# One half chunk in twelve converted on GpSimd, beside the split of x, and expert 0 in another order: a layer with sixteen experts on one core

## The chip, the core and the metric

The kernel runs on one core of one Trainium2 chip. The metric is device time in microseconds (us) of one launch; the median of three runs counts. The profile names the engines PE (TensorE's matmuls), PEld (its weight loads), DVE (VectorE), ACT (ScalarE), POOL (GpSimd) and SP (SyncE, which here only issues DMAs).

## What is computed

One transformer layer over 1024 latent tokens of width 1024 (with 256 context tokens): a combined input projection, neighbourhood attention and a gated token MLP, an output projection, and then a mixture of 16 experts in which each token goes to 2. Only the expert part and the routing ahead of it are touched here:

```python
gate = (one_hot(g_idx) ... * within ...).reshape(-1, N_EXPERTS)    # two nonzeros per token
out = jnp.zeros_like(t)
for e in range(N_EXPERTS):                                          # 16
    hid = jax.nn.silu(t @ w1[e]) * (t @ w3[e])                      # 1024 -> 512
    out = out + gate[:, e:e + 1] * (hid @ w2[e])                    # 512 -> 1024
```

## The kernel before

**Split arithmetic.** Each float32 operand of a matmul is split into a high part (rounded by a copy to the matmul's format) and a low part (the rest, by a subtraction). `mm3` issues three matmuls for each product: high by high (L86), high of x by low of the weight (L87), low of x by high of the weight (L88). Splitting x means: transpose on PE into PSUM, `hi` on ACT, `lo` on DVE.

**Weights.** An expert's weights come in six chunks of 128x2048; chunk g = 6e + c. Chunks 0 and 1 hold w1 and w3 for the first half (f=0) of the hidden columns, 2 and 3 for the second (f=1), 4 and 5 hold w2. A chunk is loaded by SP's queue into one of seven raw slots (`raw`; the one that lies in an older tile shows as `acc`), and is then converted in two halves of 128x1024: `e_hi` makes `chi` on ACT (L941), `e_lo` makes `clo` by a subtraction of two SBUF tiles (L946) on DVE or on POOL. When a chunk's conversion is through, `e_load` puts the load of chunk g+7 into the slot. The six pairs `chi`/`clo` are used in turn, so chunk g+6 overwrites chunk g.

**One expert.** The first 128 tokens of an expert are its first tile. Its rows are gathered two experts ahead into `gf` by an indirect DMA on POOL's queue, and x is split (`x_split(0)`, tiles `yhi`, `ylo`) one expert ahead. Tokens beyond 128 make a second tile (`xhi`, `xlo`, `hB`); up to 64 of them are worked with both parts stacked in one operand (`half_...`, L1401 writes its low part). How many tokens an expert has is read at run time, and the second tile's work stands in branches. In order: `x_more(e,1)` splits the second tile; `h_mm(e,0,0)` is f=0 of the first tile (24 matmuls into PSUM tile `b`); the conversion of chunks 4 and 5; `more1(e)`, all the rest of the second tile; `h_mm(e,0,1)` is f=1, with a hook after its third step; `x_split(0)` for the next expert; `gather(e+2,0)`; `y_mm` multiplies by w2 (into `yb`), its first quarter, then `h_T(0,1)`, then the rest; `y_out` scales by the gate on DVE (L1387) and adds to the output by an indirect DMA. `h_T` transposes the hidden tile `hA` on PE (L1367), with `hhi` on ACT (L1369) and `hlo` on DVE (L1370).

**PSUM.** The transposes of `h_T(0,f)` and of both halves of `x_split(0)` share two PSUM buffers of the pool `pst4` in turn: h_T(0,0) takes the first, x's first half the second, x's second half the first again, h_T(0,1) the second again. So x's second half waits for `hlo` of h_T(0,0), and h_T(0,1) waits for `ylo` of x's first half.

**What sets the order.** From the last routing tile on, every engine runs its instructions in the order in which the code is written (`manual_schedule`). Ahead of that, in the output projection and routing (`o_post`, `route`, with chunks 0 and 1 converted among them), a list scheduler orders each engine, so that a moved instruction can move others. In routing a tile's norm goes DVE, POOL (a power, L83), DVE (`hf`, L1005; logits, L1066), then a chain of small DVE operations to `mb` (L1089), which PE needs for `pr` (L1092).

**Experts by size in this input.** Experts 1, 3 to 9 and 14 have one tile; 0, 2 and 12 a half second tile; 10, 11, 13 and 15 a full second tile (15 a half third one as well).

Of the kernel before, what the change touches and what calls it, by code (L numbers as in the profile page):

```python
# [15 lines left out]
AF = mybir.ActivationFunctionType  # L16
# [12 lines left out]
E = 16  # L29
# [10 lines left out]
def hybrid_layer_kernel(ctx, tc, a, out):  # L40
    nc = tc.nc
# [43 lines left out]
    def mm3(po, xh, xl, wh, wl, first, last):  # L85
        nc.tensor.matmul(po, xh, wh, start=first, stop=False)  # L86
        nc.tensor.matmul(po, xh, wl, start=False, stop=False)  # L87
        nc.tensor.matmul(po, xl, wh, start=False, stop=last)  # L88
# [806 lines left out]
    NS, NR = 6, 7  # L895
# [5 lines left out]
    raw = [rawp.tile([P, 2048], F32, name=f"raw{i}") for i in range(3)]  # L901

    def slot_of(g):
        return g if g < 3 else g - 3 if g < 5 else g - 2 if g < 9 else slot_of(g - NR)
    sl0 = ctx.enter_context(pool("sl0"))
    chi = [sl0.tile([P, 2048], F32R, name=f"chi{i}") for i in range(2)]
# [4 lines left out]
    def e_load(g, eng=nc.sync):  # L911
        if g >= CH:
            return
        if held:
            held.append(g)
            return
        w_chunk(*divmod(g, 6), raw[slot_of(g)], eng)
# [10 lines left out]
    def e_conv(g, i, eng=None):  # L928
        if g >= CH:
            return  # L930
        e_hi(g, i)
        if eng is None:
            eng = nc.gpsimd if g == 7 or i == 1 and (g == 6 or g >= 2 * 6 and g % 6 in (0, 5)) else nc.vector
        e_lo(g, i, eng)

    def e_hi(g, i):
        sl = slice(i * 1024, (i + 1) * 1024)
        if g == 7:
            nc.vector.tensor_copy(chi[g % NS][:, sl], raw[slot_of(g)][:, sl])
        else:  # L940
            nc.scalar.activation(chi[g % NS][:, sl], raw[slot_of(g)][:, sl], AF.Copy)  # L941

    def e_lo(g, i, eng):
        sl = slice(i * 1024, (i + 1) * 1024)
        r, hi, lo = raw[slot_of(g)], chi[g % NS], clo[g % NS]
        eng.tensor_tensor(lo[:, sl], r[:, sl], hi[:, sl].bitcast(F32), op=ALU.subtract)  # L946
        if i == 1:
            e_load(g + NR if g > 1 else g + 3)

    es_r = ExitStack()  # L950
# [320 lines left out]
    for q in range(2):  # L1271
        sl = slice(q * 4, q * 4 + 4)
# [34 lines left out]
    def wk(e, c, k):  # L1307
        g = 6 * e + c
        n = 512 if c < 4 else 1024
        return chi[g % NS][:, k * n:(k + 1) * n], clo[g % NS][:, k * n:(k + 1) * n]  # L1310
# [4 lines left out]
    def bank(j, first):  # L1315
        if j:
            return psy.tile([P, 512], F32, tag="y", name="yb")
        return first.tile([P, 512], F32, tag="b", name="b")

    def bank4(j):  # L1320
        return bank(j, pst).rearrange("p (a n) -> p a n", a=4)
# [10 lines left out]
    def gather(e, j, n=P):  # L1332
        xg = (sc_f, xgi, xg2)[min(j, 2)]
        nc.gpsimd.indirect_dma_start(out=xg[0:n, :], out_offset=None, in_=hfD[:, :],  # L1334
                                     in_offset=bass.IndirectOffsetOnAxis(ap=lt[0:n, e, j, 0:1], axis=0))
        return xg

    def x_split(j):
        xg = (sc_f, xgi, xg2)[min(j, 2)]
        hi, lo = (xTi, xT0)[min(j, 1)]  # L1340
        for q in range(2):
            tr = bank4(j)
            for i in range(4):
                k = q * 4 + i
                nc.tensor.transpose(tr[:, i, :], xg[:, k * P:(k + 1) * P], ident)
            sl = slice(q * 4, q * 4 + 4)
            nc.scalar.activation(hi[:, sl, :], tr, AF.Copy)
            nc.vector.tensor_tensor(lo[:, sl, :], tr, hi[:, sl, :].bitcast(F32), op=ALU.subtract)  # L1348

    def h_mm(e, j, f, hook=None):  # L1350
        hi, lo = (xTi, xT0)[min(j, 1)]
        po = bank(j, psh)
        for k in range(KD):
            wh, wl = wk(e, 2 * f + k // 4, k % 4)
            mm3(po, hi[:, k, :], lo[:, k, :], wh, wl, k == 0, k == KD - 1)
            if hook is not None and k == hook[0]:
                hook[1]()
        h = (hA, hB)[min(j, 1)]
        nc.scalar.activation(h, po[:, 0:256], AF.Silu)
        nc.vector.tensor_tensor(h, h, po[:, 256:512], op=ALU.mult)  # L1360

    def h_T(j, f):
        hi, lo = hTs[min(j, 1)]
        h = (hA, hB)[min(j, 1)]
        tr = bank4(j)
        for i in range(2):
            nc.tensor.transpose(tr[:, i, :], h[:, i * P:(i + 1) * P], ident)  # L1367
        sl = slice(f * 2, f * 2 + 2)
        nc.scalar.activation(hi[:, sl, :], tr[:, 0:2, :], AF.Copy)  # L1369
        nc.vector.tensor_tensor(lo[:, sl, :], tr[:, 0:2, :], hi[:, sl, :].bitcast(F32), op=ALU.subtract)  # L1370

    def y_mm(e, j, k0, k1):
        hi, lo = hTs[min(j, 1)]
        if k0 == 0:
            yss[j] = [bank(1, psy) for _ in range(2)]
        for k in range(k0, k1):
            wh, wl = wk(e, 4 + k // 2, k % 2)
            for i in range(2):
                sl = slice(i * 512, (i + 1) * 512)
                mm3(yss[j][i], hi[:, k, :], lo[:, k, :], wh[:, sl], wl[:, sl], k == 0, k == 3)  # L1380

    def y_out(e, j):
        y = yo[min(j, 1)]
        gate = lt[:, e, j, 1:2].bitcast(F32)
        for i in range(2):
            sl = slice(i * 512, (i + 1) * 512)
            nc.vector.scalar_tensor_tensor(y[:, sl], yss[j][i], gate, g_f[:, sl], op0=ALU.mult, op1=ALU.mult)  # L1387
        nc.gpsimd.indirect_dma_start(out=out[:, :], out_offset=bass.IndirectOffsetOnAxis(ap=lt[:, e, j, 0:1], axis=0),  # L1388
                                     in_=y, in_offset=None, compute_op=ALU.add)
# [22 lines left out]
    def half_h(e, j, f, hook=None):  # L1412
        po = bank(1, psy)
        for k in range(KD):
            wh, wl = wk(e, 2 * f + k // 4, k % 4)
            nc.tensor.matmul(po, xT0[0][:, k, :], wh, start=k == 0, stop=False)
            nc.tensor.matmul(po, xT0[0][:, k, :], wl, start=False, stop=k == KD - 1)
            if hook is not None and k == hook[0]:
                hook[1]()
        s = xg2[0:HP, f * 512:(f + 1) * 512]  # L1420
        half_sum(s, po)
        h = hB[0:HP, :]
        nc.scalar.activation(h, s[:, 0:256], AF.Silu)
        nc.vector.tensor_tensor(h, h, s[:, 256:512], op=ALU.mult)
# [29 lines left out]
    def conv2(g):  # L1454
        for i in range(2):
            e_conv(g, i)
# [3 lines left out]
    def count(e):  # L1460
        if e <= E:
            cr[e] = nc.values_load(cnt[0:1, e:e + 1], min_val=0, max_val=T)  # L1462

    def gather_more(e):
        if e < E:
            with tc.If(cr[e] > P):
                gather(e, 1)


    def second(e, j, one, other):  # L1470
        with tc.If(cr[e] > P * j + HP) as c:
            one()
        with c.Else():
            other()

    def x_more(e, j):
        second(e, j, lambda: x_split(j), lambda: half_x(j))

    def full(e, j):
        h_mm(e, j, 1, (2, lambda: h_T(j, 0)))  # L1480
        y_mm(e, j, 0, 1)
        h_T(j, 1)
        y_mm(e, j, 1, 4)
        y_out(e, j)

    def half(e, j):
        half_h(e, j, 1, (6, lambda: half_hT(0)))
        half_y(e, j, 0, 2)
        half_hT(1)
        half_y(e, j, 2, 4)  # L1490
        half_out(e, j)
# [54 lines left out]
    for e in range(E):  # L1546
        g0 = 6 * e
        count(e + 1)
        if e == 0:
            y_mm(0, 0, 0, 4)  # L1550
            y_out(0, 0)
            gather_more(1)
            with tc.If(cr[0] > P):
                second(0, 1, lambda: h_mm(0, 1, 0), lambda: half_h(0, 1, 0))
            conv2(6)
            conv2(7)
            with tc.If(cr[0] > P):
                second(0, 1, lambda: full(0, 1), lambda: half(0, 1))
            x_split(0)
            gather(2, 0)  # L1560
            conv2(8)
            conv2(9)
            continue
        with tc.If(cr[e] > P):
            x_more(e, 1)
        h_mm(e, 0, 0)
        gather_more(e + 1)
        conv2(g0 + 4)
        conv2(g0 + 5)
        more1(e)  # L1570

        def b_hook():
            h_T(0, 0)
            conv2(g0 + 6)
        h_mm(e, 0, 1, (2, b_hook))
        if e + 1 < E:
            x_split(0)
        if e + 2 < E:
            gather(e + 2, 0)
        y_mm(e, 0, 0, 1)  # L1580
        h_T(0, 1)
        conv2(g0 + 7)
        y_mm(e, 0, 1, 4)
        conv2(g0 + 8)
        y_out(e, 0)
        conv2(g0 + 9)
# [102 lines left out]
```

## Time and profile before

| what | value |
|---|---|
| median of three runs (lowest, highest) | 1068.91 us (1068.53, 1077.0) |
| the profiled execution's own time | 1073.15 us |
| its span (first to last instruction) | 1071.3 us |
| PE busy | 1004.6 us, 94% of the span |
| DVE, ACT, POOL busy | 735.4, 536.3, 381.6 us |
| low parts made on DVE and on POOL (L946) | 160 and 32 halves |
| read from and written to HBM | 210.45 and 43.29 MB |

The span leaves out 1.85 us around the first and last instruction, and the profiled execution took 4.24 us longer than the median. Terms worked out from the trace are differences; they are added to the profiled time and to the median alike.

### The profile page before, as it was taken

Reading aid. Unit: us, or ns where it says so; the run is one execution under the profiler, and the core shown is the slowest. Engines: PE = TensorE matmul, PEld = TensorE weight load, DVE = VectorE, ACT = ScalarE, POOL = GpSimd, SP = SyncE. Lnnn points to the kernel's source line nnn. Section 1 sums busy time; section 2 is a strip of 40 time slices with the busy share of each in tenths; the row PEclk is TensorE's granted clock in tenths of the full one; section 3 lists DMA queues with packets and bytes.
Section 4 is the critical chain, followed back from the end, with each engine's and each line's share of the span. In section 5 each row is a group of like instructions: output and inputs, shape, how many; then the busy total and the mean of one; then the engine's idle time right before and its main releaser. Section 6 shows DMA issues by size and latency. Waiting matters only on the chain. (4 is left out here: it accounts for less than half of the span.)

```text
span 1071.3 us, 15841 instructions
## 1 busy us (share of the span) xinstructions
PE 1004.6 (94%) x5161; PEld 816.6 (76%) x5161; DVE 735.4 (69%) x1478; ACT 536.3 (50%) x1024; POOL 381.6 (36%) x311
## 2 busy tenths in 40 slices
PE   9999899999999999999999888999998999999992
PEld 4688787876888989988888766777776888787771
DVE  2677658874627989967776858688888654765821
ACT  4643125243527989854322437476676543554611
POOL 1130321232302565641223554435645423243510
PEclk9999999999999999999999999999999999999997
DMA  9793605876757797959342698799999996886431
GB/s 325 271 316 134 200 1 177 287 237 243 252 210 263 253 352 265 322 182 324 122 149 80 202 299 287 247 332 353 346 360 353 343 294 201 292 257 194 131 60 16
DMA packets 138118, 255.26 MB, mean 238 GB/s; under 512 B 10310, under 2 KB 86726, under 8 KB 137994
## 3 DMA queue, kind: packets, MB, share of 16 engines
q1 hardware_dynamic: 122876, 201.57, 55.7%
q0 software_dynamic: 15120, 52.19, 16.1%
q8 instruction: 60, 0.98, 0.4%
q14 instruction: 62, 0.51, 0.2%
HBM read 210.45 MB, written 43.29 MB: 237 GB/s over the span
## 5 line engine op out<-in xcount | busy, mean ns | idle before, releaser
L946 DVE TENSOR_TENSOR clo<-raw,chi 128x1024 fp32r<-128x1024 f32 x140 | 174.2, 1291 | 18.8 <-ACT chi L941 17.7
L941 ACT ACTIVATE chi<-raw 128x1024 fp32r<-128x1024 f32 x166 | 162.6, 1049 | 1.5 <-DMA raw<-in_w 1.3
L86 PE MATMUL po<-whi,hhi 128*128 128x512 f32 x352 | 146.0, 415 | 0.0
L87 PE MATMUL po<-wlo,hhi 128*128 128x512 f32 x352 | 139.6, 397 | 0.0
L88 PE MATMUL po<-whi,hlo 128*128 128x512 f32 x352 | 139.3, 396 | 0.0
L1388 POOL DMA_INDIRECT out<-xb,lt x20 | 58.0, 2899 | 152.0 <-DVE xb L1387 152.0
L86 PE MATMUL b<-chi,yhi 128*128 128x512 f32 x256 | 104.7, 409 | 7.0 <-PEq L1528 4.1
L88 PE MATMUL b<-chi,ylo 128*128 128x512 f32 x256 | 101.7, 397 | 2.0 <-DVE ylo L1348 1.6
L87 PE MATMUL b<-clo,yhi 128*128 128x512 f32 x256 | 101.3, 396 | 0.0
L83 POOL TENSOR_TENSOR ss<-ss,nhalf 128x1 f32<-128x1 f32 (+1 forms) x36 | 46.0, 1276 | 144.2 <-DVE ss L82 144.0
L946 POOL TENSOR_TENSOR clo<-raw,chi 128x1024 fp32r<-128x1024 f32 x26 | 75.2, 2899 | 52.1 <-ACT chi L941 27.8
L86 PEld LDWEIGHTS po<-whi,hhi 128*128 128x128 f32 x352 | 66.7, 189 | 16.6 <-issue 2.6
L87 PEld LDWEIGHTS po<-wlo,hhi 128*128 128x128 f32 x352 | 66.8, 190 | 16.0 <-issue 2.4
L88 PEld LDWEIGHTS po<-whi,hlo 128*128 128x128 f32 x352 | 66.7, 189 | 15.9 <-DVE hlo L218 0.3
L86 PEld LDWEIGHTS b<-chi,yhi 128*128 128x128 f32 x256 | 48.4, 189 | 23.4 <-issue 8.4
L86 PE MATMUL yb<-chi,hhi 128*128 128x512 f32 x160 | 65.7, 411 | 0.0
L88 PE MATMUL yb<-chi,hlo 128*128 128x512 f32 x160 | 62.8, 393 | 0.0
L87 PE MATMUL yb<-clo,hhi 128*128 128x512 f32 x160 | 62.6, 391 | 0.0
L88 PEld LDWEIGHTS b<-chi,ylo 128*128 128x128 f32 x256 | 48.5, 190 | 14.1 <-DVE ylo L1348 2.1
L770 DVE TENSOR_TENSOR PT<-tr,PT 128x384 fp32r<-128x384 f32 (+1 forms) x128 | 56.4, 483 | 3.3 <-ACT PT L764 3.2
L87 PEld LDWEIGHTS b<-clo,yhi 128*128 128x128 f32 x256 | 48.5, 189 | 9.6
L572 DVE CUSTOM_DVE_ANT_0 S<-S,bt 128x640 f32<-128x640 f32 x64 | 52.7, 824 | 4.2 <-DMA bt<-in_btab 3.9
(316 smaller groups left out, 2343.7 us busy)
## 6 DMA issues: line engine op xcount, KB each, us to landing
raw<-in_w SPq DMA_DIRECT2D x104, 512.0 KB, 8.2
raw<-in_w SPq DMA_DIRECT2D x27, 1024.0 KB, 9.4
wraw<-in_w_ada SPq DMA_DIRECT2D x32, 512.0 KB, 5.1
v<-vD SPq DMA_DIRECT2D x16, 768.0 KB, 6.3
bt<-in_btab SPq DMA_DIRECT2D x32, 384.0 KB, 6.8
wraw<-in_w_in SPq DMA_DIRECT2D x20, 512.0 KB, 5.4
acc<-in_w SPq DMA_DIRECT2D x18, 512.0 KB, 7.4
wada<-in_w_ada SPq DMA_DIRECT2D x16, 512.0 KB, 6.6
```

What stands on the lines that cost most here:

```text
L83: nc.gpsimd.tensor_tensor(r, r, nhalf[:, :n], op=ALU.pow)
L86: nc.tensor.matmul(po, xh, wh, start=first, stop=False)
L87: nc.tensor.matmul(po, xh, wl, start=False, stop=False)
L88: nc.tensor.matmul(po, xl, wh, start=False, stop=last)
L572: nc.vector.tensor_tensor_reduce(sv, sv, btl[t, h // 2][:, h % 2 * 384:h % 2 * 384 + LK], op0=ALU.add, op1=ALU.max, scale=1.0, scalar=-3e3 ...
L770: nc.vector.tensor_tensor(lo, tr, hi.bitcast(F32), op=ALU.subtract)
L941: nc.scalar.activation(chi[g % NS][:, sl], raw[slot_of(g)][:, sl], AF.Copy)
L946: eng.tensor_tensor(lo[:, sl], r[:, sl], hi[:, sl].bitcast(F32), op=ALU.subtract)
L1388: nc.gpsimd.indirect_dma_start(out=out[:, :], out_offset=bass.IndirectOffsetOnAxis(ap=lt[:, e, j, 0:1], axis=0), in_=y, in_offset=None, co ...
```

## The change

`e_conv` sends a low half to POOL only for the second half of a chunk with g % 6 = 0 (before: both halves of chunk 7, the second half of chunk 6, and from chunk 12 on the second half of each expert's chunks 0 and 5). So POOL makes 17 halves in place of 32, and DVE 175 in place of 160. The test now also takes chunk 0, whose conversion stands in the routing part. Chunk 7's high part, which was two copies on DVE (L939), is made on ACT like all others.

From expert 1 on, the next expert's first chunk is converted not in the hook of f=1 but in two places: its second half (ACT, then POOL) behind x_split(0), its first half (ACT, then DVE) behind h_T(0,1). The load of chunk g+7 for such a chunk is issued behind its first half. In expert 0, x_split(0) and gather(2,0) stand ahead of the second tile's second part, and chunk 7's conversion behind it. PE's instructions are the same ones; in the experts their order differs in expert 0 alone.

```diff
@@ e_conv
-            eng = nc.gpsimd if g == 7 or i == 1 and (g == 6 or g >= 2 * 6 and g % 6 in (0, 5)) else nc.vector
+            eng = nc.gpsimd if i == 1 and g % 6 == 0 else nc.vector
@@ e_hi
-        if g == 7:
-            nc.vector.tensor_copy(chi[g % NS][:, sl], raw[slot_of(g)][:, sl])
-        else:
-            nc.scalar.activation(chi[g % NS][:, sl], raw[slot_of(g)][:, sl], AF.Copy)
+        nc.scalar.activation(chi[g % NS][:, sl], raw[slot_of(g)][:, sl], AF.Copy)
@@ e_lo
-        if i == 1:
+        if i == (0 if g % 6 == 0 and g > 6 else 1):
             e_load(g + NR if g > 1 else g + 3)
@@ expert 0
             conv2(6)
-            conv2(7)
+            x_split(0)
+            gather(2, 0)
             with tc.If(cr[0] > P):
                 second(0, 1, lambda: full(0, 1), lambda: half(0, 1))
-            x_split(0)
-            gather(2, 0)
+            conv2(7)
             conv2(8)
             conv2(9)
             continue
@@ every other expert
-        def b_hook():
-            h_T(0, 0)
-            conv2(g0 + 6)
-        h_mm(e, 0, 1, (2, b_hook))
+        h_mm(e, 0, 1, (2, lambda: h_T(0, 0)))
         if e + 1 < E:
             x_split(0)
+            e_conv(g0 + 6, 1)
         if e + 2 < E:
             gather(e + 2, 0)
         y_mm(e, 0, 0, 1)
         h_T(0, 1)
+        if e + 1 < E:
+            e_conv(g0 + 6, 0)
         conv2(g0 + 7)
```

The lines behind the diff's second piece stand three lines higher in the changed kernel (L946 is L943, L1348 is L1345, and so on).

DVE in expert 1, from the low part of h_T(0,0) to `y_out`, before:

```order
L1370 TENSOR_TENSOR hlo_6688<-b,hhi_6687 128x256
L946 TENSOR_TENSOR clo_5026<-raw_6415,chi_5024 128x1024
L1360 TENSOR_TENSOR hA<-hA,b 128x256
L1348 TENSOR_TENSOR ylo_2807<-b,yhi_2806 128x512 x2
L1370 TENSOR_TENSOR hlo_6688<-b,hhi_6687 128x256
L946 TENSOR_TENSOR clo_5027<-raw_6416,chi_5025 128x1024 x2
L946 TENSOR_TENSOR clo_6419<-acc_96,chi_6418 128x1024 x2
L1387 SCALAR_TENSOR_TENSOR xb_5012<-yb,lt,gf_2801 128x512 x2
```

The same stretch of DVE after:

```order
L1367 TENSOR_TENSOR hlo_6688<-b,hhi_6687 128x256
L1357 TENSOR_TENSOR hA<-hA,b 128x256
L1345 TENSOR_TENSOR ylo_2807<-b,yhi_2806 128x512 x2
L1367 TENSOR_TENSOR hlo_6688<-b,hhi_6687 128x256
L943 TENSOR_TENSOR clo_5026<-raw_6415,chi_5024 128x1024
L943 TENSOR_TENSOR clo_5027<-raw_6416,chi_5025 128x1024 x2
L943 TENSOR_TENSOR clo_6419<-acc_96,chi_6418 128x1024 x2
L1384 SCALAR_TENSOR_TENSOR xb_5012<-yb,lt,gf_2801 128x512 x2
```

The first chunk's half on DVE has moved from ahead of `hA` and the split of x to behind the second `hlo`.

POOL in expert 0, from the conversion of chunk 6 to the gather for expert 2, before:

```order
L946 TENSOR_TENSOR clo_5026<-raw_6416,chi_5024 128x1024
L946 TENSOR_TENSOR clo_5027<-acc_96,chi_5025 128x1024 x2
L1557 COMPARE_AND_BRANCH
L1471 COMPARE_AND_BRANCH
L1388 DMA out<-xb_5013,lt 1152x1024
L1471 UNCONDITIONAL_BRANCH
L1451 DMA out<-xb_5013,lt 1152x1024
L1471 UNCONDITIONAL_BRANCH
L1557 ISA
L1557 UNCONDITIONAL_BRANCH
L1334 DMA gf_2801<-hfD,lt 128x1024
```

The same stretch of POOL after:

```order
L943 TENSOR_TENSOR clo_5026<-raw_6416,chi_5024 128x1024
L1331 DMA gf_2801<-hfD,lt 128x1024
L1555 COMPARE_AND_BRANCH
L1468 COMPARE_AND_BRANCH
L1385 DMA out<-xb_5013,lt 1152x1024
L1468 UNCONDITIONAL_BRANCH
L1448 DMA out<-xb_5013,lt 1152x1024
```

Chunk 7 has left POOL, and the gather stands ahead of the second tile's output.

POOL in the routing part, from the output of the first tile on, before:

```order
L960 CAST iota<-ioti 128x128
L995 DMA out<-x_5051 128x1024
L83 TENSOR_TENSOR r<-r,nhalf 128x1
L1006 DMA hfD<-hf 128x1024
L995 DMA out<-x_5184 128x1024
```

The same stretch of POOL after:

```order
L957 CAST iota<-ioti 128x128
L992 DMA out<-x_5051 128x1024
L943 TENSOR_TENSOR clo_5026<-raw_5018,chi_5024 128x1024
L83 TENSOR_TENSOR r<-r,nhalf 128x1
L1003 DMA hfD<-hf 128x1024
```

Half of chunk 0 now stands ahead of the first tile's power (L83). On PE the scheduler has put `pr` of that tile earlier: before, two matmuls (L86, L87) and the transposes of `z` stood ahead of it, and now they stand behind it.

## Rows read from the trace of the kernel before

**Rows 1.** Windows: stretch, length, PE, PEld, DVE, ACT, POOL busy, PEclk, DMA, GB/s.

```profile
647.80:650.00 2.20, 2.14 (x9) 1.78 (x10) 2.20 (x4) 1.93 (x3) 1.90 (x2) 1.00 0.41 32
...
740.40:760.10 19.70, 18.66 (x84) 14.41 (x84) 16.91 (x19) 13.68 (x19) 10.64 (x4) 1.00 1.07 353
...
828.00:831.40 3.40, 3.37 (x9) 2.65 (x10) 2.48 (x3) 1.80 (x2) 1.52 (x1) 0.54 1.13 305
```

**Rows 2.** Waits of PE from 600 to 1056 us: total, times, longest.

```profile
PE b L1367 <- DVE ylo L1348: 5.1, 6, 0.9
```

**Rows 3.** Timeline of expert 5: start, length, engine, instruction, idle time before it.

```profile
740.38 0.47 PE L86 MATMUL b<-chi,yhi 128*128 128x512 f32 x1
...
750.50 2.85 POOL L946 TENSOR_TENSOR clo<-acc,chi 128x1024 fp32r<-128x1024 f32 x1 [3.28 <-ACTq L1528]
...
751.96 2.48 DVE L946 TENSOR_TENSOR clo<-raw,chi 128x1024 fp32r<-128x1024 f32 x1 [0.21 <-ACT chi L941]
...
753.32 3.37 POOL L946 TENSOR_TENSOR clo<-raw,chi 128x1024 fp32r<-128x1024 f32 x1
...
755.43 0.44 PE L1367 MATMUL b<-ident,hA 128*128 128x128 f32 x2 [0.82 <-DVE ylo L1348]
...
760.17 0.47 PE L86 MATMUL b<-chi,yhi 128*128 128x512 f32 x1
```

**Rows 4.** Timeline of the second tile in expert 0, of expert 1's start and of expert 2.

```profile
633.90 3.43 DVE L939 CAST chi<-acc 128x1024 fp32r<-128x1024 f32 x2
...
637.59 0.79 PE L1440 MATMUL yb<-chi,hhi 128*128 128x512 f32 x1 [3.50 <-DVE hhi L1401]
...
646.46 0.74 DVE L1450 SCALAR_TENSOR_TENSOR xb<-yb,lt,gf 64x512 f32<-64x512 f32 x1
...
647.86 0.50 PE L88 MATMUL b<-chi,ylo 128*128 128x512 f32 x1 [1.62 <-DVE ylo L1348]
...
673.68 0.39 PE L1416 MATMUL yb<-chi,xhi 128*128 128x512 f32 x1
```

**Rows 5.** Timeline from expert 10 into expert 11, by engine (POOL, ACT, DVE, PE).

```profile
870.70 2.48 POOL L946 TENSOR_TENSOR clo<-raw,chi 128x1024 fp32r<-128x1024 f32 x1 [2.10 <-ACT chi L941]
...
872.21 1.09 ACT L1347 ACTIVATE yhi<-b 128x512 fp32r<-128x512 f32 x2
874.26 0.39 ACT L1369 ACTIVATE hhi<-b 128x256 fp32r<-128x256 f32 x1 [0.96 <-PE b L1367]
874.54 5.79 ACT L941 ACTIVATE chi<-raw 128x1024 fp32r<-128x1024 f32 x6
...
875.62 4.63 DVE L946 TENSOR_TENSOR clo<-raw,chi 128x1024 fp32r<-128x1024 f32 x4 [0.52 <-ACT chi L941]
...
883.76 1.28 DVE L1348 TENSOR_TENSOR xlo<-yb,xhi 128x512 fp32r<-128x512 f32 x2
...
885.14 0.40 PE L88 MATMUL yb<-chi,xlo 128*128 128x512 f32 x1
```

**Rows 6.** Timeline of expert 12's half second tile (DVE, PE).

```profile
919.62 0.75 DVE L1401 TENSOR_TENSOR xhi<-yb,xhi 128x256 fp32r<-128x256 f32 x2
...
926.64 1.40 DVE L1424 TENSOR_TENSOR hB<-hB,yb 64x256 f32<-64x256 f32 x1 [0.48 <-ACT hB L1423]
...
920.43 0.39 PE L1416 MATMUL yb<-chi,xhi 128*128 128x512 f32 x1
```

**Rows 7.** Timeline of the first tile's routing (POOL, DVE, PE).

```profile
492.48 1.46 POOL L83 TENSOR_TENSOR r<-r,nhalf 128x1 f32<-128x1 f32 x1 [2.80 <-DVE r L82]
...
493.98 1.29 DVE L1005 SCALAR_TENSOR_TENSOR hf<-z,r,acc 128x1024 f32<-128x1024 f32 x1 [0.46 <-POOL r L83]
...
505.00 0.16 DVE L1089 TENSOR_TENSOR mb<-M 128x16 bf16<-128x16 f32 x1
...
503.96 0.39 PE L86 MATMUL po<-woh,yhi 128*128 128x512 f32 x1
```

**Rows 8.** Timeline of PE in expert 9, between f=0 and f=1.

```profile
828.03 0.57 PE L86 MATMUL b<-chi,yhi 128*128 128x512 f32 x1 [2.47 <-PEq L1528]
```

## The prediction

> **What bounds the kernel now.** I read the page first: PE is busy 94% of the span, so only PE's waits can be won. In the experts the list of PE's waits names one that comes back in most experts with a single tile: L1367, the transposes of h_T(0,1), behind DVE's `ylo`, 6 times and 5.1 us in all [rows 2]. The timeline of expert 5 shows how it arises: PE stands 0.82 us at 755.43 [rows 3]. Ahead of `hA` and `ylo` on DVE is the first chunk's half of 751.96, which took 2.48 us, where four in a row take 4.63, or 1.16 each [rows 5]. It began while POOL's half of 750.50 (2.85 us, to 753.35) was running, and what it took beyond 1.16 ends there. POOL's next half, of 753.32, took 3.37 us in place of 2.48 alone [rows 3, 5]: it waited for DVE in turn. So the two engines' subtractions from SBUF exclude each other: a half on POOL keeps the next half on DVE waiting until it is done. The window of that expert shows DVE busy 16.91 of 19.70 us [rows 1], in one queue in which the order decides who waits. The second place is expert 0: two copies on DVE take 3.43 us beside POOL, PE waits 3.50 us for what is queued behind them, and then 1.62 us for `ylo` at the start of expert 1 [rows 4].
>
> **The routing part: 2.7 us lost.** Half of chunk 0 goes to POOL, ahead of the first tile's power. That power starts at 492.48 [rows 7], and DVE's operations ahead of it read two SBUF tiles. With 2.48 us of POOL [rows 5] from about 490.5, they and the power end some 1.3 us later, and `hf` with them. Behind `hf` DVE now has both halves of chunk 1, one more than before (1.16), while o_post operations of about 1.0 us have moved from ahead of `mb` to behind it: `mb` comes 1.3 + 1.16 - 1.0 = 1.4 us later, at 505.16 + 1.4 = 506.55. PE reaches the new place of `pr` at 503.96 [rows 7] and waits 2.6 us; two matmuls and a late `z` follow, and I put the loss at 2.7. PE is full from there to the experts, so nothing gives it back. Its ends are 0 (the power is not delayed) and 4.0 (the clock falls as well, below); I take the worked-out value.
>
> **Experts 0 to 2: 3.4 us won.** With the copies on ACT and chunk 7 behind the second tile, PE's wait of 3.50 us shrinks to about 1.1 (`hhi` now waits for the split of x on ACT and DVE), and the half clock behind it goes, some 1.3 us (nine matmuls took 3.40 us at clock 0.54 against 2.20 at 1.00 [rows 1]; the waits are compared below). The transposes of x, 0.8, come earlier on the same path. So DVE ends the second tile's output not at 646.46 + 0.74 = 647.2 but 3.1 earlier, at 644.1 [rows 4]. From there DVE is what sets the pace, because it has all of chunks 7, 8 and 9 to make: 6 halves (6.9) to 651.0; `hA`, 4 halves and `hlo` (0.4 + 4.63 + 0.4; the like-sized `hhi` takes 0.39) to 656.45; then x's second half, its `yhi`, one `chi` and POOL's half, 0.4 + 0.55 + 1.05 + 2.48 = 4.5; then 7 halves and `y_out`, 9.3; then the first half of expert 2's split, 0.4: 671.05. PE needs it where it now runs at 673.68 [rows 4]: 2.6 won. A further 0.8 comes in expert 2, where `hB` no longer waits for POOL (the same operation takes 1.40 us in expert 12 [rows 6], and at most half of that by its size). Bounds: nothing if DVE falls further behind, and 6.4 if every wait named here went and none came (3.50 + 1.3 + 1.62).
>
> **The six experts with one tile: 1.2 us won.** Moving the half behind the second `hlo` frees h_T(0,1), so 0.85 us each could go, 5.1 at most. But POOL's half of chunk 5 now lies on DVE ahead of `hlo` of h_T(0,0), and x's second half needs the buffer that this `hlo` frees. DVE's own round is 0.4 + 4.63 + 0.4 = 5.4 to that `hlo`, 4.5 to the end of POOL's half as above, 9.3 for 7 halves and `y_out`: 19.2 us, and the round is now 760.17 - 740.38 = 19.79 [rows 3]. Without any wait PE would need 18.9. So DVE becomes the bound at 19.2 or, with gaps between its instructions, a little more: the wait moves from h_T(0,1) to x's second half. I take 0.2 each, six times; ends: 5.1 won, 1 lost.
>
> **The second tiles: 8.0 us lost.** Here PE does not wait today, since the second tile gives DVE time. In expert 10 `yhi` ends at 872.21 + 1.09 = 873.30 [rows 5]. In the new order comes one `chi` (1.05) to 874.35, then POOL's half to 876.83. DVE's half of the same chunk is ready at about 875.75 (behind `hhi`, 0.39, and a second `chi`, 0.97) and waits for POOL, as in expert 5. It ends at 878.0. What follows ran from 875.62 to 883.76, 8.14 us for six halves and `y_out`; so `xlo` starts not at 883.76 but at 886.15, and its first half ends at 886.8. PE wanted it at 885.14: a wait of 1.7 us. The same order stands ahead of experts 10, 11, 13 and 15: 6.8 us. If POOL's half did not hold DVE the wait would be about 0.5 each; I take 1.7, since expert 5's rows are the very case. In expert 12 L1401 began at 919.62 and PE followed at 920.43 [rows 6]; 2.4 us later it costs 2.0, less 0.8 for `hB` without POOL beside it: 1.2.
>
> **Edits at nothing.** chi of chunk 7 on ACT lies beside DVE's output of the second tile. The loads of chunks are issued up to 3 us later against PE, because the halves that free their slots are; they lie behind loads still in flight in the experts with one tile, and elsewhere DMA has room. If that cover is gone, ACT waits, up to 2 us once. The earlier gather(2,0) can only land earlier. The last expert has nothing to convert and ends as before.
>
> **The sum.** 2.7 - 3.4 - 1.2 + 6.8 + 1.2 = 6.1 us. The profiled execution would go from 1073.15 to 1079.25; the median from 1068.91 to 1075.0, 0.6% slower. One per cent, 10.7 us, is about what a measurement of this kernel can tell from no change.
>
> **Rivals.** *A: DVE is never late, and the waits simply go.* For it: POOL loses 15 of 32 halves, and what DVE did beside it took up to twice as long. Against: the counts above, above all the single `xlo` that PE takes 0.7 us after it is made today. It would win 6.4 + 5.1 = 11.5 us: 1057.4. The stretch of expert 5 moves 353 GB/s [rows 1]. [...]
>
> [...]
>
> *C: the new waits come out at half.* POOL's half starts later than I think, or DVE gets in first, so a second tile costs 0.5 to 0.9, and the routing chain is hidden by the scheduler: 3.4 + 1.2 won against about 4: no change, 1068.
>
> **Chances.** Forecast 0.58 (1070 to 1080), A 0.10, B 0.17, C 0.15. Range 1064 to 1083: it reaches to C whole and nearly to B, and leaves out A and the far end of B. Faster by over 1%: 0.06, the outer half of A. Slower by over 1%: 0.19, B and the upper edge of the forecast. Within: 0.75.
>
> **What the profile of the changed kernel would show.** POOL with 17 halves; L1367 (L1364 there) no longer waiting for `ylo`, but the transposes of x waiting for `hlo` in experts 4 to 8, with rounds of 19.2 to 19.8 us; PE waiting about 1.7 us for `xlo` in experts 10, 11, 13 and 15; `pr` waiting for `mb` at about 504; expert 2's second tile starting 2.6 us earlier against the start of the experts. I am wrong if DVE's half behind the second `hlo` does not wait for POOL, if PE shows no wait for `xlo`, or if branch waits like that of rows 8, which no edit touches, fall otherwise.

## The result: 0.7% slower, and the profile after

The changed kernel takes 1077.26 us (median; 1074.31 to 1083.53), the kernel before 1071.22 us in the runs beside it (1065.81 to 1077.0). The ratio is 1.0073, 95% interval 1.0055 to 1.0091: 5.9 to 9.7 us slower. That is inside the prediction's range and within the 1% that it took for no change, though the interval leaves out a ratio of 1. The profiled execution took 1077.07 us.

The page of the changed kernel: the span, and each engine's busy time, its share and its instructions.

```profile
span 1075.3 us, 15833 instructions
...
PE 1003.0 (93%) x5161; PEld 813.9 (76%) x5161; DVE 751.7 (70%) x1491; ACT 541.0 (50%) x1026; POOL 356.6 (33%) x296
```

PE's waits from 600 us to the end (total, times, longest), to be read beside [rows 2]. Line numbers are three lower than before: L1342 transposes x, L1364 the hidden tile, L1398 is the low part of a half second tile.

```profile
PE b L1342 <- DVE hlo L1367: 6.9, 7, 1.3
PE yb L86 <- DVE xlo L1345: 6.7, 4, 1.9
PE yb L1413 <- DVE xhi L1398: 4.2, 3, 1.7
PE yb L1437 <- DVE hhi L1398: 3.9, 5, 0.9
PE b L86 <- PEq L1525: 3.6, 2, 2.8
```

The wait of L1364 for `ylo` is gone. In its place x's second half waits for `hlo` seven times, and the second tiles wait for `xlo` and for the half tile's low part, 6.7 + 4.2 us that were 0.8 before. The four waits for `xlo` are 1.89, 1.93, 1.94 and 0.94 us, in experts 10, 11, 13 and 15.

Expert 5 in the changed kernel, to be read beside [rows 3].

```profile
737.22 0.47 PE L86 MATMUL b<-chi,yhi 128*128 128x512 f32 x1
...
747.42 2.35 DVE L943 TENSOR_TENSOR clo<-acc,chi 128x1024 fp32r<-128x1024 f32 x2
749.99 0.42 DVE L1367 TENSOR_TENSOR hlo<-b,hhi 128x256 fp32r<-128x256 f32 x1 [0.21 <-DVEq L1525]
...
750.47 0.66 PE L1342 MATMUL b<-ident,gf 128*128 128x128 f32 x4 [0.89 <-DVE hlo L1367]
...
752.85 2.42 POOL L943 TENSOR_TENSOR clo<-raw,chi 128x1024 fp32r<-128x1024 f32 x1 [6.73 <-ACT chi L938]
...
753.24 0.42 DVE L1367 TENSOR_TENSOR hlo<-b,hhi 128x256 fp32r<-128x256 f32 x1 [0.69 <-ACT hhi L1366]
754.19 3.30 DVE L943 TENSOR_TENSOR clo<-raw,chi 128x1024 fp32r<-128x1024 f32 x2 [0.52 <-ACT chi L938]
...
757.00 0.47 PE L86 MATMUL b<-chi,yhi 128*128 128x512 f32 x1
```

Chunk 5's second half now lies on DVE (747.42) ahead of `hlo`, and PE stands 0.89 us for it. The round, from PE's first product in one expert to its first in the next, is 757.00 - 737.22 = 19.78 us, as before. The row at 753.24 tells what POOL excludes: `hlo`, which reads one operand from PSUM, takes its usual 0.42 us while POOL's half runs. The two halves behind it, which read two SBUF tiles, take 3.30 instead of 2.35: the first ended about 1.1 us after POOL's (755.27), that is, it had waited. The same holds wherever POOL's half starts first in this trace: in all 15 pairs the half of DVE that meets it ends 1.08 or 1.09 us after POOL's, where one alone takes 1.21.

From expert 10 into expert 11, to be read beside [rows 5].

```profile
870.51 2.41 POOL L943 TENSOR_TENSOR clo<-raw,chi 128x1024 fp32r<-128x1024 f32 x1 [5.74 <-ACT chi L938]
...
871.80 6.75 DVE L943 TENSOR_TENSOR clo<-raw,chi 128x1024 fp32r<-128x1024 f32 x5 [0.52 <-ACT chi L938]
...
882.06 1.28 DVE L1345 TENSOR_TENSOR xlo<-yb,xhi 128x512 fp32r<-128x512 f32 x2
...
882.89 0.47 PE L86 MATMUL yb<-chi,xhi 128*128 128x512 f32 x1 [1.93 <-DVE xlo L1345]
```

DVE's five halves take 6.75 us, 0.95 more than five in a row, because the first waits for POOL; behind eight more instructions `xlo` is late, and PE stands 1.93 us.

The first tile's routing, to be read beside [rows 7].

```profile
487.40 2.48 POOL L943 TENSOR_TENSOR clo<-raw,chi 128x1024 fp32r<-128x1024 f32 x1
...
487.57 2.86 DVE L984 TENSOR_TENSOR z<-x,gf 128x512 f32<-128x512 f32 x1
...
490.49 0.66 PE L1016 MATMUL tr<-ident,z 128*128 128x128 f32 x4 [1.26 <-DVE z L984]
...
502.67 0.17 DVE L1086 TENSOR_TENSOR mb<-M 128x16 bf16<-128x16 f32 x1
```

POOL's half holds `z`, a product of two SBUF tiles, for 2.2 us, and PE waits 1.26 for it. `z` is another tile than POOL's `clo`, so no order between the two halves of one chunk can be what holds it. The forecast had PE wait 2.6 us for `mb` here; in the trace `pr` starts at 503.11 with no idle time of PE before it.

`hB` in expert 12, whose two operands also lie in SBUF, took 1.40 us beside POOL's half [rows 6]. POOL has no half there now:

```profile
926.71 0.42 DVE L1421 TENSOR_TENSOR hB<-hB,yb 64x256 f32<-64x256 f32 x1 [0.48 <-ACT hB L1420]
```

PE at the same wait in expert 13:

```profile
954.91 0.47 PE L86 MATMUL yb<-chi,xhi 128*128 128x512 f32 x1 [1.94 <-DVE xlo L1345]
```

And the window right behind it, with the granted clock third from the end:

```profile
956.50:959.80 3.30, 3.30 (x10) 2.59 (x9) 3.30 (x4) 0.68 (x1) 0.00 (x0) 0.52 1.10 364
```

The granted clock stands at 0.52 for 3.3 us, and a matmul of 128x512 takes 0.63 us there, where it takes 0.39 at clock 1.00; some 1.6 us are lost, an estimate from 3.3 x 0.48. It is the only one of the four waits for `xlo` with that behind it: the clock is 1.00 in 844.90:849.00, 882.80:887.00 and 1014.60:1019.00, behind the other three.

**Where the time went.** Worked out from the starts of PE's first product in each expert, in the two profiled executions (spans 1071.3 and 1075.3):

| part | forecast | measured, us |
|---|---|---|
| ahead of routing, the same work | 0 | -2.3 |
| first routing transposes of z to expert 0 | +2.7 | +0.9 |
| experts 0 to 2 | -3.4 | -3.0 |
| experts 4 to 8, and 14 (one tile) | -1.2 | +0.7, +1.4 |
| experts 3 and 9 (branch waits, clock) | | +1.2, -3.1 |
| second tiles of 10, 11, 13, 15 | +6.8 | +1.8, +2.1, +2.1, +1.1 |
| half clock in expert 13 | 0 | +1.7 |
| expert 12 | +1.2 | +1.1 |
| behind f=1 of expert 15 | 0 | -1.7 |
| sum | +6.1 | +4.0 |

The parts that the change does not touch (the first row, the last, the branch waits and the clock) differ by some us from one execution to the next. Without the first and the last row the sum is 8.0, near the 7.8 of the ratio; without the row on the clock as well it is 6.3, so the agreement is partly luck.

The clock can be set apart, since span and granted clock of every run are known. Their product is an estimate of the time at full clock, as if PE filled the span. Its mean is 1061.4 us over the 19 runs of the changed kernel (clock 0.986) and 1051.8 to 1052.8 over the three sets of runs of the kernel before (0.983 to 0.984). By that estimate the change costs some 9 us, and a higher clock gives back some 2.

**The branch waits.** The prediction named waits of PE's sequencer between f=0 and f=1, at a run-time branch, that no edit touches. The trace of the DMA packets shows what comes ahead of their end. In expert 3 of the changed kernel PE stands from 701.86 on:

```profile
704.61 0.47 PE L86 MATMUL b<-chi,yhi 128*128 128x512 f32 x1 [2.75 <-PEq L1525]
```

From 702.06 to 703.04 one packet of 16 KB with instructions comes in. The DMA queues in the window 702.0:703.1 show it:

```profile
q8 instruction: 1, 0.02, 5.6%
```

In all fourteen profiles the branch waits of over 0.5 us in experts 3 and 9 (26 of them) have such a packet, and PE starts again 1.56 to 1.60 us after its end (1.41 in one). In the kernel before it is 1.59 us in expert 3 and 1.58 in expert 9 (waits of 1.61 and 2.47), in the changed one 1.57 in both (2.75 and 0.82). What was measured is this order, with nearly the same time between the two; that PE waits for the load is read from it. Why the load starts when it does is not shown: 1.36 us before PE stood in expert 3 of the kernel before, 0.20 us after it in the changed one.

### The profile page after: what moved, and what is told of

Read it like the earlier page. It is cut to its first block, busy times and chain, and to the rows that moved or that the text cites. A ratio compares the mean times of both kernels' runs of the same rounds, so it can differ in the third digit from the quotient of the medians.

```text
span 1075.3 us, 15833 instructions
## 1 busy us (share of the span) xinstructions
PE 1003.0 (93%) x5161; PEld 813.9 (76%) x5161; DVE 751.7 (70%) x1491; ACT 541.0 (50%) x1026; POOL 356.6 (33%) x296
## 5 line engine op out<-in xcount | busy, mean ns | idle before, releaser
L943 DVE TENSOR_TENSOR clo<-raw,chi 128x1024 fp32r<-128x1024 f32 x151 | 189.3, 1304 | 8.2 <-ACT chi L938 8.2
L86 PE MATMUL po<-whi,hhi 128*128 128x512 f32 x352 | 145.3, 413 | 0.0
L87 PE MATMUL po<-wlo,hhi 128*128 128x512 f32 x352 | 139.3, 396 | 0.0
L86 PE MATMUL b<-chi,yhi 128*128 128x512 f32 x256 | 104.0, 406 | 6.3 <-PEq L1525 3.6
L87 PE MATMUL b<-clo,yhi 128*128 128x512 f32 x256 | 100.7, 393 | 0.9 <-DVE clo L943 0.9
L83 POOL TENSOR_TENSOR ss<-ss,nhalf 128x1 f32<-128x1 f32 (+1 forms) x36 | 45.9, 1276 | 142.0 <-DVE ss L82 141.9
L86 PEld LDWEIGHTS po<-whi,hhi 128*128 128x128 f32 x352 | 66.4, 189 | 16.2 <-issue 2.2
L87 PEld LDWEIGHTS po<-wlo,hhi 128*128 128x128 f32 x352 | 66.6, 189 | 15.6 <-issue 2.2
L86 PE MATMUL yb<-chi,hhi 128*128 128x512 f32 x160 | 65.6, 410 | 0.0
L86 PEld LDWEIGHTS b<-chi,yhi 128*128 128x128 f32 x256 | 48.1, 188 | 22.6 <-issue 8.8
L87 PE MATMUL yb<-clo,hhi 128*128 128x512 f32 x160 | 62.7, 392 | 0.0
L943 POOL TENSOR_TENSOR clo<-raw,chi 128x1024 fp32r<-128x1024 f32 x15 | 36.4, 2428 | 74.1 <-ACT chi L938 74.0
L87 PEld LDWEIGHTS b<-clo,yhi 128*128 128x128 f32 x256 | 48.2, 188 | 10.9 <-DVE clo L943 1.3
## 6 DMA issues: line engine op xcount, KB each, us to landing
raw<-in_w SPq DMA_DIRECT2D x27, 1024.0 KB, 10.5
```

The costliest lines, as they stand in the source:

```text
L83: nc.gpsimd.tensor_tensor(r, r, nhalf[:, :n], op=ALU.pow)
```

## The experiments

The theory was the prediction's: a half on POOL and a DVE subtraction of two SBUF tiles exclude each other, so the place of POOL's half decides who is late. The rival: DVE is late by its number of halves. Ratios are against the kernel before, with 95% intervals. The code is shortened, and "..." stands for what is left out.

**Expert 0's part alone**, twice (chunk 7's high part is on ACT too, as in the change):

```diff
-            eng = nc.gpsimd if g == 7 or i == 1 and (g == 6 or ...) else nc.vector
+            eng = nc.gpsimd if i == 1 and (g == 6 or ...) else nc.vector
...
             conv2(6)
-            conv2(7)
+            x_split(0); gather(2, 0)
             with tc.If(cr[0] > P): second(0, 1, full..., half...)
-            x_split(0); gather(2, 0)
+            conv2(7)
```

> The kernel before with expert 0's part of the change alone (chunk 7's conversion as that of every other chunk, and the split of x ahead of the second tile, chunk 7 behind it); everything else as before. The prediction gave this part 3.4 us, with ends 0 and 6.4; against the start of the experts the profile of the changed kernel shows 3.0 to 4.3 us won up to expert 3. So, if the part is worth what it shows there and nothing later takes it back: 3 to 4 us faster than the kernel before, ratio 0.996 to 0.997. If DVE's later work or the weights' loads take it back in the next experts: 0 to 1 us, ratio 0.999 to 1.000.

> Expert 0's part alone, once more: its profile showed nothing won beyond expert 1, its times 0.9945. If the times stand, 0.993 to 0.997 again, and more of the second profile is at full clock; if they were luck, 0.998 to 1.000.

Measured: 0.9945 (0.9921 to 0.9968) and 0.9947 (0.9917 to 0.9977), 5.8 us faster, more than the 3.4. The profile of the first does not show that gain: its list of PE's waits has

```profile
PE b L1364 <- DVE ylo L1345: 5.3, 6, 1.1
...
PE b L1342 <- DVE hlo L1367: 3.1, 1, 3.1
```

The second row is a new wait in expert 1, and from the start of the experts to expert 4 both profiles of this version (114.9 and 116.6 us) stand no better than the one of before (114.3). What the times add is for the most part clock: its mean over the runs is 0.988 and 0.987, against 0.984 and 0.983 in the runs of the kernel before beside them. By the estimate of span times clock (1051.7 and 1051.2 against 1052.6 and 1052.8 us) 4.4 and 4.0 us are the clock, and 0.9 and 1.6 all the rest. The next run, which keeps the old expert 0, fits that.

**The steady change alone** (expert 0 and chunk 0 as before):

```diff
-            eng = nc.gpsimd if i == 1 and g % 6 == 0 else nc.vector
+            eng = nc.gpsimd if g == 7 or i == 1 and g % 6 == 0 and g > 0 else nc.vector
... (the other experts as in the change)
```

> The changed kernel with expert 0 and chunk 0 put back as before, so only the change in the experts 1 to 15 is left (one half of twelve on GpSimd beside the split of x, the first half moved behind the second hlo). The prediction gave it -1.2 + 6.8 + 1.2 = 6.8 us lost; by the profile of the changed kernel, experts 3 to 15 lose some 8.4 us, of which 1.4 is a stretch at half clock. So 7 to 8.4 us slower than before, ratio 1.0065 to 1.008. If the waits for xlo are made up elsewhere (rival C), under 4 us. If these waits cost the clock each time (rival B), over 11.

Measured: 1.0085 (1.0064 to 1.0106), 9.1 us slower; the first theory's 7 to 8.4 lie within the interval. In the window behind the old wait for `hhi` in expert 0 this execution lost about 5 us by the clock (an estimate from 10.5 x 0.49):

```profile
632.00:642.50 10.50, 8.60 (x24) 6.34 (x25) 3.99 (x8) 1.88 (x4) 5.19 (x2) 0.51 0.66 223
```

The half clock began within the wait of 3.51 us (629.69 to 633.20) and stood for 10.2 us. In the execution of before that was one stretch of 3.4 us, 1.3 us by the prediction. So the old order of expert 0 costs between one and three such stretches; no profile with the new order has one at that place.

**Chunk 0 back on DVE:**

```diff
-            eng = nc.gpsimd if i == 1 and g % 6 == 0 else nc.vector
+            eng = nc.gpsimd if i == 1 and g % 6 == 0 and g > 0 else nc.vector
```

> The changed kernel with one half of chunk 0 back on DVE, ahead of the routing; all else as changed. The prediction put the loss there at 2.7 us, with ends 0 and 4.0. The changed profile shows z held for 2.86 in place of 0.69 us by GpSimd's half, and PE waiting 1.66 us for it, and nearly no wait for mb. So 1.4 us faster than the changed kernel, that is 5.5 to 6.5 us slower than before; if the prediction's 2.7 holds, 4 to 5 us slower than before; if PE's wait is covered anyway, as slow as the changed kernel.

Measured: 1.0044 (1.0026 to 1.0062), median 1077.24. `z` takes 0.68 us again. (The 1.66 us in the expectation are no row of the profile; the wait for `z` there is 1.26.) So the routing part is 3 us by the two ratios, whose intervals overlap, and nothing by the medians; by the profile (the stage in the table) and by span times clock it is 1. The times alone do not settle it.

**No half on POOL beside the split of x:**

```diff
-            eng = nc.gpsimd if i == 1 and g % 6 == 0 else nc.vector
+            eng = nc.gpsimd if i == 1 and g in (0, 6) else nc.vector
```

> The changed kernel, with the half of the first chunk on DVE in place of GpSimd from chunk 12 on (GpSimd converts nothing in experts 1 to 15 but half of chunk 6 in expert 0). If DVE's half waits for GpSimd's to end, as the prediction has it, the two halves take 2.3 us of DVE in place of 2.48 + 1.16: xlo of the second tiles comes about 1.1 to 1.3 us earlier, and their wait falls from about 1.9 to 0.7 each; the rounds of experts 4 to 9 fall from 19.8 to 20.1 to about 19.0 to 19.3. That makes some 8 to 10 us against the changed kernel, about the time of before or 2 us less. If the two engines work beside each other and DVE is late by its own count of halves, DVE has 1.16 us more in each expert: 1.16 x 4 second tiles and up to 1.16 x 6 single ones, 5 to 11 us slower than the changed kernel.

Measured: 0.9981 (0.9963 to 0.9999). DVE has more to do, and PE waits for it less:

```profile
PE yb L86 <- DVE xlo L1345: 3.6, 4, 0.9
...
PE b L1342 <- DVE hlo L1367: 2.0, 6, 0.8
```

The four waits for `xlo` fall from 6.7 to 3.6 us in all and the rounds of experts 4 and 5 to 19.25 us. That speaks for the exclusion and against the count.

**Which half POOL takes.** Three versions with expert 0 as changed and chunk 0 on DVE: POOL has both halves in the changed order, only chunk 0's (of the next expert) in the order of before, or only chunk 5's in the changed order.

```diff
 # both, changed order (against the changed kernel)
+            eng = nc.gpsimd if i == 1 and (g == 6 or g >= 2 * 6 and g % 6 in (0, 5)) else nc.vector
 # first chunk only, order of before
+            eng = nc.gpsimd if i == 1 and g % 6 == 0 and g > 0 else nc.vector
+        h_mm(e, 0, 1, (2, lambda: (h_T(0, 0), conv2(g0 + 6))))
 ...
 # sixth chunk only, changed order
+            eng = nc.gpsimd if i == 1 and (g == 6 or g >= 2 * 6 and g % 6 == 5) else nc.vector
```

> The changed order in every expert, with chunk 0's half on DVE, and with the half of the sixth chunk of each expert back on GpSimd: GpSimd has two halves an expert as before, only their places are the changed ones. Tells the two parts of the steady change apart, from the run with expert 0's part alone (0.9945) and the run of everything but the routing part (1.0044). If what costs is that GpSimd's half now stands beside the split of x, ahead of DVE's half of the same chunk (the order), the waits for xlo stay at 1.9 us and the ratio at 1.002 to 1.0045. If what costs is that DVE has one half more (1.16 us an expert), the waits for hlo and xlo go back and the ratio falls to 0.993 to 0.997.

> Expert 0 as changed and the order in the other experts as before (both halves of the first chunk behind the first hlo); of the steady change only the half of the sixth chunk on DVE in place of GpSimd. If the order is what costs, this stays within 2 us of the run with expert 0's part alone (0.9945): 0.993 to 0.997, with no wait for xlo. If DVE's extra half is what costs, it comes ahead of ylo and hA in each expert and the ratio is 1.001 to 1.006.

> The changed order with GpSimd's one half of an expert taken from the sixth chunk and not from the first: nothing stands on GpSimd beside the split of x, and DVE has as many halves as in the changed kernel. If DVE's half waits for GpSimd's, this beats the run without any half on GpSimd (0.9981), since DVE has one half less there: the waits for xlo shrink to 0 to 0.9 us, the rounds of one tile come to 18.9 to 19.2 us, and the ratio to 0.993 to 0.997. If the number of DVE's halves decides, it is like the changed kernel: 1.003 to 1.007.

Measured: 1.0098 (1.0061 to 1.0135), 0.9994 (0.9972 to 1.0016) and 0.9989 (0.9966 to 1.0011). The first lies outside both expectations. It is no faster than the run with chunk 0 back on DVE (1.0044, and the intervals just touch), though DVE has a half less: the waits for `xlo` stay at 1.9 us, as the order would have it, and POOL's half of chunk 5 now also holds the half that stands ahead of `hlo`.

```profile
725.33 2.46 POOL L943 TENSOR_TENSOR clo<-raw,chi 128x1024 fp32r<-128x1024 f32 x1 [1.17 <-ACTq L1525]
...
725.45 3.41 DVE L943 TENSOR_TENSOR clo<-raw,chi 128x1024 fp32r<-128x1024 f32 x1
...
729.56 0.66 PE L1342 MATMUL b<-ident,gf 128*128 128x128 f32 x4 [1.92 <-DVE hlo L1367]
```

The third has as many halves on DVE as the run with chunk 0 back on DVE (1.0044), and their intervals lie apart: the place decides, not the number.

The second lies between the two expectations, some 5 us slower than expert 0's part alone by the times; its mean clock, 0.984 against 0.988, makes up some 3.8 of them by the estimate above. Its profile shows how near the two engines come to each other. In experts 4, 5, 7 and 8 DVE's half of the first chunk starts 0.15 us ahead of POOL's and is not held, and the rounds are 19.3 to 19.6 us, below the 19.8 to 20.1 of expert 0's part alone: the extra half costs nothing there. In expert 6 (and in expert 3) POOL starts 0.21 us ahead: in expert 6 DVE's half takes 3.26 us, PE waits 2.06 us for `ylo` with half clock behind it (0.52 in 777.0:780.5), and the round is 23.6 us. Expert 5, then expert 6:

```profile
752.80 1.22 DVE L943 TENSOR_TENSOR clo<-raw,chi 128x1024 fp32r<-128x1024 f32 x1
...
752.96 3.31 POOL L943 TENSOR_TENSOR clo<-raw,chi 128x1024 fp32r<-128x1024 f32 x1 [5.75 <-ACT chi L938]
...
772.53 2.38 POOL L943 TENSOR_TENSOR clo<-acc,chi 128x1024 fp32r<-128x1024 f32 x1 [5.96 <-ACT chi L938]
...
772.74 3.26 DVE L943 TENSOR_TENSOR clo<-acc,chi 128x1024 fp32r<-128x1024 f32 x1
...
776.99 0.56 PE L1364 MATMUL b<-ident,hA 128*128 128x128 f32 x2 [2.06 <-DVE ylo L1345]
```

How often that happens in other executions is not known.

The third has rounds of 18.9 us in experts 4 to 7, as hoped, but not the ratio. In expert 10 PE waits 4 us for `xlo`, behind an ACT that waits for a load, and the clock stands at half for 6.8 us after it:

```profile
838.89 2.01 ACT L938 ACTIVATE chi<-raw 128x1024 fp32r<-128x1024 f32 x2 [2.23 <-DMA raw<-in_w]
...
846.68 0.77 PE L86 MATMUL yb<-chi,xhi 128*128 128x512 f32 x1 [3.98 <-DVE xlo L1345]
```

**Only DVE's half moved**, POOL's two halves where they were before:

```diff
         def b_hook():
             h_T(0, 0)
-            conv2(g0 + 6)
+            e_conv(g0 + 6, 1)
...
         h_T(0, 1)
+        e_conv(g0 + 6, 0)
```

> Expert 0 as changed; in the other experts GpSimd has its two halves where it had them before (half of the sixth chunk, half of the next first chunk behind the first hlo), and only DVE's half of that chunk is moved behind the second hlo, as in the change. It takes the half that GpSimd held for 2.48 us from ahead of ylo without putting a GpSimd half beside the split of x. By the reading that GpSimd's half holds DVE's subtractions from SBUF and no others, PE's waits for ylo (5 us in the run with expert 0's part alone) go and no wait for xlo comes: 3 to 5 us faster than that run, ratio 0.990 to 0.992. If DVE is late by its number of halves, the wait moves on to the second half of x and the ratio stays at 0.994 to 0.996.

Measured: 0.9969 (0.9951 to 0.9987), not the 0.990 to 0.992. The waits for `ylo` in experts 4 to 8 are gone and the rounds are about 18.7 us, but the stretch from expert 4 to expert 10 is hardly shorter (122.2 before). Its windows, whole, then experts 4 to 8 and expert 9:

```profile
723.23:844.49 121.26, 114.46 (x512) 90.02 (x513) 98.20 (x112) 87.09 (x111) 57.20 (x25) 0.97 1.07 353
...
723.23:817.15 93.92, 92.23 (x420) 72.79 (x421) 78.49 (x90) 69.40 (x89) 48.26 (x20) 1.00 1.07 350
817.15:844.49 27.34, 22.23 (x92) 17.23 (x92) 19.71 (x23) 17.69 (x22) 8.94 (x5) 0.88 1.06 364
```

The rounds are 5% shorter, yet the bytes per us in them are no more than before (350 GB/s; 353 before [rows 1]): the loads fall behind. ACT and PE in expert 9, where the gain goes:

```profile
834.00 1.06 ACT L938 ACTIVATE chi<-raw 128x1024 fp32r<-128x1024 f32 x1 [3.90 <-DMA raw<-in_w]
...
836.59 0.69 PE L1364 MATMUL b<-ident,hA 128*128 128x128 f32 x2 [3.94 <-DVE ylo L1345]
```

Of the 4.2 us that expert 9 takes longer than before, part is clock: it stands at half for 6.8 us behind that wait, for 3.4 us before.

**With half of the loads of w1 and w3 left out in experts 4 to 9**, in this version and in expert 0's part alone:

```diff
-            for i, w in enumerate(("w1", "w3")):
+            for i, w in enumerate(("w1", "w3")[0:1 if 4 <= e < 10 else 2]):
```

> The version with only DVE's half moved (two halves on GpSimd, expert 0 as changed), and with half of each load of w1 and w3 left out in experts 4 to 9, so that the output is not the reference's there. In the full version the rounds of experts 4 to 8 fell to 18.7 us, but expert 9 then waited 3.9 us for ylo, behind a chunk whose load was late. If the loads set the pace of experts 4 to 9, with a third of the bytes gone the rounds stay at 18.7 and the wait in expert 9 goes: some 5 to 7 us faster than the full version, ratio 0.990 to 0.992. If that wait has another cause (the branch, the order on DVE), it stays, and the ratio is that of the full version, 0.995 to 0.998.

> Expert 0's part alone, with the same loads left out (the output is not the reference's there either). If the order on DVE and GpSimd alone sets the rounds of experts 4 to 8 there, they stay at 19.8 us with ylo waited for in each, and the time is that of the full version (0.9945) or 1 to 2 us less by expert 9. If it is the loads, the rounds fall to about 18.9 us and the ratio to 0.988 to 0.991.

Measured: 0.9934 (0.9906 to 0.9962) and 0.9956 (0.9931 to 0.9981). With fewer bytes the first keeps its rounds of 18.7 us and has no wait for `ylo` in expert 9; the same stretch takes 115.3 us in place of 121.3:

```profile
721.27:836.61 115.34, 111.11 (x513) 88.24 (x513) 95.55 (x109) 84.72 (x109) 59.23 (x25) 1.00 0.93 295
```

The second keeps rounds of 19.8 us and its waits for `ylo` (6.1 us in all). So in the order of before it is DVE and POOL that set these rounds, and the loads stand so close behind that most of what is won there is lost again. By the times the step of 3.5 thousandths is not certain (the intervals overlap); the profile shows it.

**Expert 1 mended as well**, from expert 0's part alone:

```diff
         def b_hook():
             h_T(0, 0)
-            conv2(g0 + 6)
+            if e > 1: conv2(g0 + 6)
...
         x_split(0)
+        if e == 1: e_conv(g0 + 6, 1, nc.vector)
...
         h_T(0, 1)
+        if e == 1: e_conv(g0 + 6, 0)
```

> Expert 0 as changed, and in expert 1 alone the first chunk of the next expert converted behind the split of x and behind the second hlo, both halves on DVE; from expert 2 on all as before. In the profile of expert 0's part alone PE waits 3.1 us in expert 1 for hlo, with a stretch at half clock behind it, and has lost there all that expert 0 won; with the changed order that wait is 1.0 us. If that is a loss by itself, this run wins 3 to 4 us over expert 0's part alone: ratio 0.990 to 0.992. If the weights' loads of experts 3 to 9 set the time there, as two further runs test, only what the clock gives back is kept: 0.993 to 0.995.

Measured: 0.9945 (0.9921 to 0.9969), no better than expert 0's part alone. The wait for `hlo` in expert 1 falls from 3.1 to 0.9 us, but the branch in expert 3 waits 3.1 us. Of the versions with all their loads none beats expert 0's part alone by its times; this one equals it.

## Why the prediction was right, point by point

The forecast of 6.1 us lies near the 7.8 of the ratio, and the mechanism behind its largest term is shown. That the sum came so near is partly luck: the term for the routing was some 1.7 us too high, that for the experts with one tile some 3.3 too low, and the clock, which moves the time by several us, was in no term of the sum but that of experts 0 to 2.

- **The mechanism.** Right. In these traces POOL's half and DVE's subtractions of two SBUF tiles exclude each other: the row of `z` (2.86 for 0.69 us), that of expert 11 (6.75 for 5.80) and the run without POOL (waits for `xlo` of 3.6 for 6.7) show it; an instruction with a PSUM operand was not held (`hlo`, 0.42 us beside POOL's half and without it). The one that came first took its usual time, and the other was longer: where POOL came first (2.4 us) DVE's half took 2.1 to 3.4 us for 1.21, and where DVE came first (1.22) POOL's took 3.3 for 2.4.
- **Second tiles, +6.8.** Right in place and in the sum: 6.7 us in the list of waits, three of 1.9 and one of 0.9 in place of four of 1.7; 7.1 in the starts. Expert 12, +1.2: measured 1.1.
- **One-tile experts, -1.2.** The wait moved from `ylo` to x's second half, as forecast; the size was off: +2.1. The term that was mis-sized is "DVE's own round is 0.4 + 4.63 + 0.4 = 5.4 to that `hlo`, 4.5 to the end of POOL's half as above, 9.3 for 7 halves and `y_out`: 19.2 us". In expert 5 of the changed kernel the three parts are 5.6 (744.81 to 750.41), 4.9 (to 755.27) and 9.35 us (to the next `hA` at 764.62). The rounds came out at 19.8 to 20.2, and the wait in expert 5 at 0.89 us in place of 0.2.
- **Routing, +2.7.** Mis-sized: about 1 by the profiles. The step that failed is "With 2.48 us of POOL [rows 5] from about 490.5": POOL's half ran from 487.40, in a stage that began 2.3 us earlier, so 0.8 us sooner than assumed. It held `z`, and PE waited for `z`; but the power and `hf` (490.77 and 491.36) came within 0.6 us of their old places, and `mb`, at 502.67 for 505.00, did not move within the stage.
- **Experts 0 to 2, -3.4.** Right by the profile up to expert 3 (3.0); expert 2's second tile starts 2.4 us earlier against the start of the experts (2.6 forecast). The working has two slips that almost cancel: 3.50 - 1.1 + 1.3 - 0.8 is 2.9 and not 3.1, and the chain from 644.1 on ends at 670.65 and not 671.05; put right, the term would be 2.9 for 2.6. By the times the part is worth 5.8, of which the runs' clock makes up 4 or more by the estimate above; the term for the clock behind the wait of 3.50 us [rows 4] was put at one stretch, 1.3 us, and can be three (10.2 us in the run of the steady change).
- **Rival A** failed twice: the waits did not go, and where they do go (experts 4 to 9) the loads take over. In all versions with full loads the DMA engines move 349 to 354 GB/s from expert 4 to expert 10, with a busy share of 1.06 to 1.07, and from expert 4 to expert 11 the time is 156.4 to 160.6 us. That these rates are the most the core can get is not shown: expert 9 in the run with only DVE's half moved has 364 over 27 us. Nor do they hold single rounds at 19.8 us: five rounds of that run took 18.7, and the loads fell behind until expert 9 waited for them.
- **Rival B**, that the new waits cost PE its clock as well, happened once: a wait of 1.94 us had half clock behind it in expert 13 (0.52), waits of 1.89 and 1.93 in experts 10 and 11 of the same execution had not (1.00). A branch wait of 2.75 us in expert 3 of that execution (704.61) had not either (1.00 in 704.60:709.00). So in these runs the length of the wait alone does not decide. With waits for `xlo` of up to 1.9 and 2.0 us, one execution of the steady change had half clock in expert 10 (0.50 in 851:853), one with chunk 0 back on DVE in expert 11 (0.50 in 886:888).
- **Branch waits** were named as what no edit touches, and their falling otherwise as a sign of being wrong. It came: the rounds with them changed by +1.2 and -3.1 us, 1.7 of the latter clock. PE goes on there 1.57 to 1.59 us behind an instruction load, as shown above; no term of the sum had them.

## What to carry to other kernels

Give GpSimd work that overlaps with VectorE instructions reading PSUM (`hlo` took 0.42 us beside its half and without it), and look at what stands behind the VectorE instruction that its half will hold (here a subtraction of two SBUF tiles took 2.1 to 3.4 us for 1.21); a half taken from GpSimd wins nothing if the one left stands in the wrong place (17 halves in place of 32, and 0.7% slower). Before mending a wait that returns in every round, look how close behind the transfers stand: here 5.2 us won in five rounds were all but lost in the sixth (4.2 us), because the loads came no faster (350 and 353 GB/s). A single long wait can cost more by the clock behind it than by itself: in one execution 3.5 us of waiting, and then 10.2 us at half clock, about 5 us by the estimate above.

## What the runs showed that was not expected

The same wait of 3.5 us in expert 0 was followed by half clock for 3.4 us in one execution and for 10.2 us in another. The run-time branch between f=0 and f=1 cost up to 3.1 us, with an instruction load that ended 1.6 us before PE went on (1.57 to 1.59 in the profiles of the two kernels). The part ahead of the experts, which no version touches but through chunk 0, ended between 600.4 and 610.5 us in fourteen profiles, with two to six stretches at half clock in each: single profiles of this kernel cannot rank versions that differ by less than that, and only stages compared by their own starts do.
